# The overflow block of a mixture of experts, taken into the expert pairs: gate beside up in the two halves of the array

## The chip, the cores and the metric

The kernel runs on one core of one Trainium2 chip. The metric is the time of one execution on the device, in microseconds (us); lower is better. Of several runs the median counts.

## The reference

The model has two layers. Each mixes the tokens (attention beside a recurrent branch) and then sends every token through a hierarchical mixture of experts: 4 groups of 8 experts, the best group of a token, and the best two experts in it. In layer 0 all 512 tokens (256 of context, 256 latent) go through the experts, in layer 1 the 256 latent ones alone. The weights are of one layer; D_MODEL is 1024, an expert's hidden width 256, and everything is float32.

```
def hier_moe(h, w_rg, b_rg, w_re, b_re, w_e_gate, w_e_up, w_e_down):
...
    w_top = w_top / w_top.sum(-1, keepdims=True) * p_grp
    eid = grp[..., None] * EXPERTS_PER_GROUP + i_top
    comb = jnp.einsum('bnk,bnke->bne', w_top, jax.nn.one_hot(eid, N_EXPERTS, dtype=F32))
    y = jnp.zeros_like(h)
    for g in range(N_GROUPS):
        sl = slice(g * EXPERTS_PER_GROUP, (g + 1) * EXPERTS_PER_GROUP)
        a = jnp.einsum('bnd,edf->bnef', h, w_e_gate[sl])
        u = jnp.einsum('bnd,edf->bnef', h, w_e_up[sl])
        hid = jax.nn.silu(a) * u * comb[..., sl, None].astype(h.dtype)
        y = y + jnp.einsum('bnef,efd->bnd', hid, w_e_down[sl])
    return y
...
    for l in range(DEPTH):
...
            xc = layer_norm(DEEPNORM_ALPHA * xc + g2c * hier_moe(modulate(xc, sh2c, sc2c), *moe_args),
                            ln2_g[l], ln2_b[l])
        xl = layer_norm(DEEPNORM_ALPHA * xl + g2l * hier_moe(modulate(xl, sh2l, sc2l), *moe_args),
                        ln2_g[l], ln2_b[l])
```

## The kernel before, in words

Each layer is `mixer(l)` and then `moe(l)`. In `moe` every expert owns 64 slots, and a token takes a slot in each of its two experts. Tokens that find their expert full go to overflow blocks, 64 slots of one expert each; layer 0 always runs one such block, the first, and every further one stands behind a condition. Two experts make a pair. The weights of a pair, 6 MiB, lie in six tiles of 1 MiB: four of gate and up, two of down.

The loop over the 16 pairs j is written so that PE (TensorE) goes through it in the order of the code (`manual_schedule`). An iteration does this:

- `load` issues the four tiles of gate and up of pair j on SP's queue;
- `up` (L1438) multiplies the transposed tokens of both experts, 64 columns of the array for each, so that the matmuls of the two experts run abreast in the two halves of the array. A row of the program is one f32 matmul; in the trace it is two rows. The 512 output columns are gate and up side by side;
- `fetch(j + 2)`: `who` (L1426, DVE) finds which tokens are in the slots of the pair two further on, and `gather` (L1394, POOL) fetches them from HBM into one of three tiles `xr`;
- `finish` of the pair before: `place` builds the matrix Pm that puts slots back to tokens (L1415 and L1416, DVE), `load_down` issues its two tiles of down weights, and `down` (L1461) multiplies and splits the result into a high and a low part, yh (L189, ACT) and yl (L190, DVE);
- `turn(j + 1)` transposes the fetched tokens of the next pair (L1406, eight transposes);
- every second iteration `combine` begins for the two pairs finished by then: for each of 8 outputs (4 token tiles by 2 halves of D_MODEL) four matmuls, yh and yl of either pair (L1475, L1476), then DVE scales (L1478) and POOL adds to X (L1484). Four outputs are done in an iteration;
- `hidden` transposes the products silu(gate) times up (L1449).

After iteration j = 3 of layer 0 the block runs by itself: `extra(0, self.wm)` takes three weight tiles from the ring, fills them by indirect DMA on POOL's queue (L1347, tile `wx`), and goes through `who`, `gather`, `turn`, `up`, `hidden`, `down` and `combine` with one expert. Its `up` and `down` use one half of the array, and its `combine` is 16 matmuls over 64 slots.

The weight tiles go round in a ring, `self.wm`. It has four tiles of the whole kernel (`NW`) and `NW2` more during `moe`: 7 in layer 0 (11 in all), 9 in layer 1 (there the tile `X01` is taken in as well, 14 in all). A load waits until the tile that it overwrites has been read by its last matmul. The first loads of a layer are issued before the mixer has ended, as many as the ring has tiles.

After layer 0's experts, the weights `wada` of the next layer's modulation take over the ring (L382 multiplies by them), beside the layer norm of each token tile on DVE.

Of the kernel before, what the change touches and what calls it, by code (L numbers as in the profile page):

```python
# [83 lines left out]
class Kern:  # L84
# [199 lines left out]
    def run(self):  # L284
        tc, nc, I = self.tc, self.nc, self.I
        with ExitStack() as ctx:
            self.cp = ctx.enter_context(tc.tile_pool(name="const", bufs=1))
            self.wp = ctx.enter_context(tc.tile_pool(name="wslots", bufs=self.NW))
            self.dp = ctx.enter_context(tc.tile_pool(name="dram", bufs=1, space=bass.MemoryType.DRAM))
            self.cur = self.cp  # L290
            self.setup()
            for l in range(L):
                self.l = l
                self.PSB = {"g": 2, "a": 3, "t": 2, "d": 1}
                self.half, self.wi = None, -1
                self.NU = 34 if l == L - 1 else 40
                with tc.tile_pool(name=f"mix{l}", bufs=1, reuse_waits="tile") as self.mp, \
                        tc.tile_pool(name=f"psx{l}", bufs=1, space=bass.MemoryType.PSUM, reuse_waits="tile") as self.pp:
                    self.cur = self.mp
                    self.mixer(l)  # L300
                if self.stop == f"mix{l}":
                    return
                self.PSB = {"g": 1, "a": 2, "t": 2, "d": 3}
                self.NW2 = 9 if l == L - 1 else 7
                self.spare = [self.X01] if l == L - 1 else []
                with tc.tile_pool(name=f"moe{l}", bufs=1, reuse_waits="tile") as self.ep, \
                        tc.tile_pool(name=f"psm{l}", bufs=1, space=bass.MemoryType.PSUM, reuse_waits="tile") as self.pp:
                    self.cur = self.ep
                    self.moe(l)
                if self.stop == f"moe{l}":  # L310
                    return
# [984 lines left out]
    def moe(self, l):  # L1296
# [90 lines left out]
        def gather(tok, m, x=None):  # L1387

            ti = sm([128, 1], "ti", I32)
            if x is None:  # L1390
                x = xrs[xi[0] % 3]
                xi[0] += 1
            nc.vector.tensor_scalar(ti, tok, 512.0, None, op0=OP.add)
            nc.gpsimd.indirect_dma_start(out=x[0:m], out_offset=None, in_=self.h2_d[l],  # L1394
                                         in_offset=bass.IndirectOffsetOnAxis(ap=ti[0:m], axis=0),
                                         bounds_check=N - 1, oob_is_err=False)
            return x
# [69 lines left out]
        def combine(parts, sums=None):  # L1467

            for i, t in enumerate(QT):
                for h in range(2):  # L1470
                    hs = slice(h * 512, h * 512 + 512)
                    p = self.ps("d")
                    for j, (Pm, yh, yl, m) in enumerate(parts):
                        lt = Pm[0:m, i * 128:i * 128 + 128]
                        nc.tensor.matmul(p, lhsT=lt, rhs=yh[h][0:m], start=(j == 0), stop=False)  # L1475
                        nc.tensor.matmul(p, lhsT=lt, rhs=yl[h][0:m], start=False, stop=(j == len(parts) - 1))  # L1476
                    a = self.pm(name="acc") if sums else ep.tile([128, 512], F32, tag="acc", name="acc", bufs=2)
                    nc.vector.tensor_tensor(out=a, in0=p, in1=g2[t // 2][h], op=OP.mult)  # L1478
                    X = self.X[t][:, hs]
# [7 lines left out]
        def stats(X, nm, eps):  # L1487

            v, a, r = (self.ss_tile([128, 2], x) for x in "var")
            q, v, a, r = v[:, 1:2], v[:, 0:1], a[:, 0:1], r[:, 0:1]  # L1490
            xi[0] += 1
            nc.scalar.activation(xrs[xi[0] % 3], X, AF.Square, bias=nm, accum_out=q)
            nc.vector.tensor_scalar(v, q, 0.5 / D, 0.5 * eps, op0=OP.mult, op1=OP.add)
            self.newton(r, v, a)
            return r

        def extra(ob, new=None):

            W, Wd = load_indexed(ob, new)
            tok, ws = who(NSTAT + 64 * ob, "" if new else "x")  # L1500
            xs = turn(gather(tok, 64, None if new else xrs[2]), 64)
            yh, yl = down(hidden(up(xs, W, 1, ws), 1), Wd, 1)
            self.drain(combine([(place(NSTAT + 64 * ob), yh, yl, 64)]))

# [28 lines left out]
        got[1] = fetch(1)  # L1535
        with tc.manual_schedule(engines={eng.PE}):
            xs = turn(got[0][1], 128)
            for j in range(E // 2):
                W = load([2 * j, 2 * j + 1])
                ws, _ = got.pop(j)  # L1540
# [2 lines left out]
                    got[j + 2] = fetch(j + 2)  # L1543
                if hid:
                    finish(hid)
                if j + 1 < E // 2:
                    xs = turn(got[j + 1][1], 128)
                if len(done) == 2 or last and done and j == E // 2 - 1:
                    self.drain(comb)
                    comb = combine(done)  # L1550
                    done = []
                for _ in range(n):
                    next(comb, None)
                hid = hidden(si, 2), j
                if j == 3:
                    self.drain(comb)
                    if not last:
                        extra(0, self.wm)
        finish(hid)
        ln2 = self.wm("ln2")  # L1560
        for i, nm in enumerate(("ln2_g", "ln2_b")):
# [46 lines left out]
```

## Time and profile before

| | |
|---|---|
| median of 3 runs | 1428.43 us (1427.02 to 1432.36) |
| profiled execution | 1431.51 us, of which the span of the trace is 1429.4 us |
| mean granted TensorE clock | 0.947 of full speed |
| PE busy | 1294.4 us of the span |
| layer 0, experts | PE's first `up` at 541.88 us, last `combine` ends at 824.4 us |
| layer 1, experts | from 1177.3 us to the end |

Times in the trace count from the start of its span; the 2.1 us by which the execution is longer lie outside. PEclk in a row is the share of TensorE's full clock that was granted in that stretch; DMA is the mean busy share of the 16 DMA engines. In a timeline, a row is a run of like instructions: its start, its length from first start to last end, the engine, the line, the operation, the tile written and the tiles read, the shape and the count, and in square brackets the time for which the engine sat idle before and what ended that.

### The profile page before, as it was taken

The numbers are of one execution on the slowest core, as the hardware profiler recorded it, in microseconds if no ns is written. First come the engines' busy times: TensorE is split into PE (matmuls) and PEld (weight loads), VectorE is DVE, ScalarE is ACT, GpSimd is POOL, SyncE is SP. The second block draws the span as 40 slices with busy tenths as digits, with TensorE's granted clock in tenths as the row PEclk, the third lists the DMA queues.
The fourth block names the chain that finished last, engine by engine and source line by source line (L and its number), as shares of the span: only waits on it lengthen the run. The fifth ranks groups of instructions, "written<-read, shape, count | busy, mean of one in ns | idle before, by whom it ended". The sixth has DMA issues, their size and how long they took to land. (4 is left out here: it accounts for less than half of the span.)

```text
span 1429.4 us, 19667 instructions
## 1 busy us (share of the span) xinstructions
PE 1294.4 (91%) x6839; PEld 834.8 (58%) x6839; DVE 794.9 (56%) x2189; ACT 451.2 (32%) x998; POOL 377.7 (26%) x385
## 2 busy tenths in 40 slices
PE   5899999999999828999999959999999749999995
PEld 1788867776776623444454517898878634444342
DVE  3745777553236945555554486478775863343325
ACT  3534344443340102111121137356545212121121
POOL 1310114100343302444343212112524401232222
PEclk9999999999999858989999989999999959999998
DMA  9633464211247567979999968321444768999994
GB/s 326 207 114 131 145 214 140 82 30 59 89 177 269 168 256 250 403 264 409 408 407 409 403 211 278 96 81 39 152 143 132 237 250 329 408 408 406 407 409 158
DMA packets 145970, 339.64 MB, mean 238 GB/s; under 512 B 21552, under 2 KB 67792, under 8 KB 145856
## 3 DMA queue, kind: packets, MB, share of 16 engines
q1 hardware_dynamic: 137184, 322.61, 61.7%
q0 software_dynamic: 6224, 10.31, 2.1%
q10 hardware_dynamic: 2448, 5.31, 1.0%
q8 instruction: 59, 0.97, 0.3%
q14 instruction: 55, 0.45, 0.1%
HBM read 344.62 MB, written 4.29 MB: 244 GB/s over the span
## 5 line engine op out<-in xcount | busy, mean ns | idle before, releaser
L1438 PE MATMUL ps_g<-we,xs 128*64 128x512 f32 x992 | 243.7, 617 | 6.6 <-DMA we<-in_w_e_up 4.2
L1438 PEld LDWEIGHTS ps_g<-we,xs 128*64 128x64 f32 x992 | 76.3, 141 | 148.2 <-issue 141.6
L160 POOL TENSOR_TENSOR wsl<-wc,wsh 128x512 fp32r<-128x512 f32 x54 | 72.5, 1346 | 321.7 <-ACT wsh L176 284.1
L1484 POOL TENSOR_TENSOR X<-X,acc 128x512 f32<-128x512 f32 x96 | 125.2, 1327 | 109.8 <-DVE acc L1478 109.7
L160 DVE TENSOR_TENSOR wsl<-wc,wsh 128x512 fp32r<-128x512 f32 x108 | 84.5, 786 | 98.3 <-ACT wsh L176 87.0
L176 ACT ACTIVATE wsh<-wc 128x512 fp32r<-128x512 f32 x162 | 99.0, 628 | 118.6 <-PE ps_g L197 81.1
L1442 DVE SCALAR_TENSOR_TENSOR si<-si,ws,ps_g 128x256 f32<-128x256 f32 (+1 forms) x33 | 15.8, 480 | 211.4 <-ACT si L1441 211.4
L1461 PE MATMUL ps_a<-we,hidT 128*64 128x512 f32 x496 | 125.3, 595 | 2.1 <-DMA we<-in_w_e_down 1.9
L1394 POOL DMA_INDIRECT xr<-h2d,ti x33 | 34.9, 1057 | 315.2 <-PE ps_t L1406 207.2
L196 PE MATMUL ps_g<-hTh,wsh 128*128 128x512 f32 (+1 forms) x320 | 112.4, 351 | 2.0 <-ACT tg L639 2.0
L197 PE MATMUL ps_g<-hTl,wsh 128*128 128x512 f32 (+1 forms) x320 | 111.1, 347 | 0.0
L198 PE MATMUL ps_g<-hTh,wsl 128*128 128x512 f32 (+1 forms) x320 | 110.6, 346 | 0.0
L196 PE MATMUL ps_g<-wsh,hTh 128*128 128x256 f32 x368 | 105.5, 289 | 2.5 <-ACT v L599 2.4
L197 PE MATMUL ps_g<-wsl,hTh 128*128 128x256 f32 x368 | 104.2, 284 | 0.0
L198 PE MATMUL ps_g<-wsh,hTl 128*128 128x256 f32 x368 | 103.7, 283 | 0.0
L382 PE MATMUL ps_d<-wada,sT 128*32 128x512 f32 x380 | 70.3, 645 | 29.5 <-DMA wada<-in_w_ada 29.4
L1478 DVE TENSOR_TENSOR acc<-ps_d,g 128x512 f32<-128x512 f32 x108 | 74.1, 689 | 38.0 <-PE ps_d L1476 21.9
L1441 ACT ACTIVATE si<-ps_g 128x256 f32<-128x256 f32 (+1 forms) x33 | 12.7, 384 | 245.7 <-PE ps_g L1438 179.0
L1475 PE MATMUL ps_d<-yh,pmr 128*128 128x512 f32 (+1 forms) x200 | 83.7, 419 | 0.4 <-DVE acc L1478 0.2
L1461 PEld LDWEIGHTS ps_a<-we,hidT 128*64 128x64 f32 x496 | 38.6, 137 | 76.1 <-issue 62.8
L1476 PE MATMUL ps_d<-yl,pmr 128*128 128x512 f32 (+1 forms) x200 | 80.2, 403 | 0.9 <-DVE yl L190 0.9
L196 PEld LDWEIGHTS ps_g<-wsh,hTh 128*128 128x128 f32 x368 | 69.6, 190 | 9.2 <-ACT v L599 2.6
(420 smaller groups left out, 2710.3 us busy)
## 6 DMA issues: line engine op xcount, KB each, us to landing
we<-in_w_e_gate SPq DMA_DIRECT2D x124, 512.0 KB
we<-in_w_e_up SPq DMA_DIRECT2D x124, 512.0 KB
we<-in_w_e_down SPq DMA_DIRECT2D x124, 512.0 KB
wada<-in_w_ada SPq DMA_DIRECT2D x95, 512.0 KB
wc<-in_w_in SPq DMA_DIRECT2D x63, 512.0 KB
wc<-in_w_out SPq DMA_DIRECT2D x16, 512.0 KB
wc<-in_w_bo_mla SPq DMA_DIRECT2D x8, 512.0 KB
wc<-in_w_bo_mlstm SPq DMA_DIRECT2D x6, 512.0 KB
```

What stands on the lines that cost most here:

```text
L160: eng.tensor_tensor(out=out, in0=a, in1=b, op=OP.subtract)
L176: self.nc.scalar.activation(view(hi), src, AF.Copy)
L196: self.nc.tensor.matmul(out, lhsT=ah, rhs=bh, start=(i == 0), stop=False)
L197: self.nc.tensor.matmul(out, lhsT=ah, rhs=bl, start=False, stop=False)
L198: self.nc.tensor.matmul(out, lhsT=al, rhs=bh, start=False, stop=(i == n - 1))
L382: nc.tensor.matmul(ps[32 * c:32 * c + 32], lhsT=self.sT[:, kb], rhs=wt[c // 2][:, (c % 2) * 512:(c % 2) * 512 + 512], start=(kb == 0), sto ...
L1438: nc.tensor.matmul(p[64 * e:64 * e + 64], lhsT=xs[:, k, 64 * e:64 * e + 64], rhs=W[e, k], start=(k == 0), stop=(k == 7))
L1461: nc.tensor.matmul(p[64 * e:64 * e + 64], lhsT=hT_[:, c, 64 * e:64 * e + 64], rhs=W[e, c, h], start=(c == 0), stop=(c == 1))
L1475: nc.tensor.matmul(p, lhsT=lt, rhs=yh[h][0:m], start=(j == 0), stop=False)
L1476: nc.tensor.matmul(p, lhsT=lt, rhs=yl[h][0:m], start=False, stop=(j == len(parts) - 1))
L1478: nc.vector.tensor_tensor(out=a, in0=p, in1=g2[t // 2][h], op=OP.mult)
L1484: nc.gpsimd.tensor_tensor(out=X, in0=X, in1=a, op=OP.add)
```

## The change

The block of layer 0 is no longer a step of its own. A class `First` does its parts inside the iterations: `ask` (who and gather) in iteration 1, `place` and `up` in iteration 3 ahead of `hidden`, `down` in iteration 4 behind `finish`, and its result is a third part of the `combine` that starts in iteration 4. Its `up` puts gate (256 columns) into one half of the array and up into the other. Its `down` multiplies the same slots in both halves, so that the high part of the result lies in the rows 0 to 63 of one tile, and the low part in the rows 64 to 127; `combine` then needs one matmul over 128 rows for each output. The ring gets one tile more in either layer. The gathers of the pairs go round in two tiles `xr` in place of three, and the argument `dynamic_dma_scratch_size` is set to 4096.

```
-                self.NW2 = 9 if l == L - 1 else 7
+                self.NW2 = 10 if l == L - 1 else 8
...
-                x = xrs[xi[0] % 3]
+                x = xrs[xi[0] % 2]
...
-                        nc.tensor.matmul(p, lhsT=lt, rhs=yl[h][0:m], start=False, stop=(j == len(parts) - 1))
+                        end = j == len(parts) - 1
+                        nc.tensor.matmul(p, lhsT=lt, rhs=yh[h][0:m], start=(j == 0), stop=(end and yl is None))
+                        if yl is not None:
+                            nc.tensor.matmul(p, lhsT=lt, rhs=yl[h][0:m], start=False, stop=end)
...
+        class First:
+            def ask(o):
+                o.tok, o.ws = who(NSTAT, "x")
+                o.x = gather(o.tok, 64, xrs[2])
+
+            def place(o):
+                o.P = ep.tile([128, N], F32R, tag="pmx", name="pmx", bufs=1)
...
+            def up(o):
+                W, o.Wd = o.w
+                xs = turn(o.x, 64)
+                p = self.ps("a")
+                for k in range(8):
+                    for i in range(2):
+                        nc.tensor.matmul(p[64 * i:64 * i + 64, 0:256], lhsT=xs[:, k, 0:64], rhs=W[0, k][:, i],
+                                         start=(k == 0), stop=(k == 7))
+                o.si = sm([128, 256], "si", bufs=2)
+                nc.scalar.activation(o.si[0:64], p[0:64, 0:256], AF.Silu)
+                nc.vector.tensor_scalar(o.si[0:64], o.si[0:64], o.ws[0:64], None, op0=OP.mult)
+                nc.vector.tensor_copy(o.si[64:128], p[64:128, 0:256])
+
+            def down(o):
+                t = self.ps("t")
+                for c in range(2):
+                    nc.tensor.transpose(t[:, c * 128:c * 128 + 128], o.si[:, c:256:2], self.ident)
+                tv = t[:, 0:256].rearrange("p (c g s) -> p c g s", c=2, g=2)
+                hT_ = sm([128, 2, 128], "hidT", bufs=2)[:, :, 0:64]
+                nc.scalar.activation(hT_, tv[:, :, 0], AF.Copy)
+                nc.vector.tensor_tensor(out=hT_, in0=tv[:, :, 1], in1=hT_, op=OP.mult)
+                o.y = [self.st(F32R, "yx") for h in range(2)]
+                for h in range(2):
+                    p = self.ps("a")
+                    for c in range(2):
+                        for i in range(2):
+                            nc.tensor.matmul(p[64 * i:64 * i + 64], lhsT=hT_[:, c], rhs=o.Wd[0, c, h],
+                                             start=(c == 0), stop=(c == 1))
+                    y = o.y[h]
+                    nc.scalar.activation(y, p, AF.Copy)
+                    nc.vector.tensor_tensor(out=y[64:128], in0=p[64:128], in1=y[64:128].bitcast(F32), op=OP.subtract)
+                return o.P, o.y, None, 128
...
+            fb = None if last else First()
...
+                if fb and j == 1:
+                    fb.ask()
+                if fb and j == 4:
+                    done.append(fb.down())
...
-                if len(done) == 2 or last and done and j == E // 2 - 1:
+                if len(done) >= 2 or last and done and j == E // 2 - 1:
...
+                if fb and j == 3:
+                    fb.w = load_indexed(0, self.wm)
+                    fb.place()
+                    fb.up()
                 hid = hidden(si, 2), j
-                if j == 3:
-                    self.drain(comb)
-                    if not last:
-                        extra(0, self.wm)
...
-    nc = bacc.Bacc("TRN2", target_bir_lowering=False, num_devices=1)
+    nc = bacc.Bacc("TRN2", target_bir_lowering=False, num_devices=1, dynamic_dma_scratch_size=4096)
```

On PE, before, from `hidden` of pair 3 in layer 0 to `up` of pair 4 (after the last row shown, seven more outputs of the block's combine, two matmuls each, and then `up`):

```order
L1449 MATMUL ps_t<-ident,si 128x128 x2
L1406 MATMUL ps_t<-ident,xr 128x64 x8
L1438 MATMUL ps_g<-wx,xs 64x512 x8
L1449 MATMUL ps_t<-ident,si 128x64 x2
L1461 MATMUL ps_a<-wx,hidT 64x512 x4
L1475 MATMUL ps_d<-yh,pmr 128x512
L1476 MATMUL ps_d<-yl,pmr 128x512
```

On PE, of the change, from the block's `up` in iteration 3, behind its `turn`, to the first output of the combine in iteration 4 (L1476 and L1478 are the lines 1475 and 1476 of before):

```order
L1530 MATMUL ps_a<-wx,xs 64x256 x16
L1449 MATMUL ps_t<-ident,si 128x128 x2
L1438 MATMUL ps_g<-we,xs 64x512 x16
L1461 MATMUL ps_a<-we,hidT 64x512 x8
L1540 MATMUL ps_t<-ident,si 128x128 x2
L1550 MATMUL ps_a<-wx,hidT 64x512 x8
L1406 MATMUL ps_t<-ident,xr 128x128 x8
L1476 MATMUL ps_d<-yh,pmr 128x512
L1478 MATMUL ps_d<-yl,pmr 128x512
L1476 MATMUL ps_d<-yh,pmr 128x512
L1478 MATMUL ps_d<-yl,pmr 128x512
L1476 MATMUL ps_d<-yx,pmx 128x512
```

The block's `up` now stands ahead of `hidden` of pair 3, its `down` directly behind `down` of pair 3, and its share of the combine is a fifth matmul for each of 8 outputs (four in iteration 4, four in iteration 5).

On SP, before, the loads around the point where the tiles of the ring are used up for the first time in layer 0 (the branch belongs to the condition on further blocks; PE_49 is a wait for a matmul):

```order
L1320 DMA we<-in_w_e_gate 128x1024 [waits DMAHW0_49]
L1320 DMA we<-in_w_e_up 128x1024 [waits DMAHW1_49]
L1529 UNCONDITIONAL_BRANCH
L1320 DMA we<-in_w_e_gate 128x1024 [waits DMAHW2_49,PE_49]
L1320 DMA we<-in_w_e_up 128x1024 [waits DMAHW3_49]
```

On SP, of the change, the same place:

```order
L1320 DMA we<-in_w_e_gate 128x1024 [waits DMAHW0_49]
L1320 DMA we<-in_w_e_up 128x1024 [waits DMAHW1_49]
L1320 DMA we<-in_w_e_gate 128x1024 [waits DMAHW2_49]
L1320 DMA we<-in_w_e_up 128x1024 [waits DMAHW3_49]
L1581 UNCONDITIONAL_BRANCH
L1320 DMA we<-in_w_e_gate 128x1024 [waits DMAHW4_49,PE_49]
L1320 DMA we<-in_w_e_up 128x1024 [waits DMAHW5_49]
```

One gate and up tile more, two loads of 512 KB, stands ahead of the branch and waits for no matmul.

## Rows read from the trace of the kernel before

**Rows 1.** The page, first part: busy time of each engine.

```profile
PE 1294.4 (91%) x6839; PEld 834.8 (58%) x6839; DVE 794.9 (56%) x2189; ACT 451.2 (32%) x998; POOL 377.7 (26%) x385
```

**Rows 2.** Windows: us, busy time of five engines, PEclk, DMA share, GB/s.

```profile
634.05:797.45 163.40, 163.40 (x784) 80.91 (x780) 86.47 (x179) 33.17 (x65) 62.61 (x50) 1.00 1.03 404
...
824.40:860.40 36.00, 20.34 (x113) 4.53 (x112) 29.76 (x102) 12.65 (x24) 4.36 (x4) 0.81 0.64 221
...
1240.60:1400.80 160.20, 156.47 (x706) 67.63 (x704) 53.47 (x144) 31.52 (x63) 36.75 (x30) 1.00 1.03 407
```

**Rows 3.** Timeline of PE, pairs 3 to 5 of layer 0: start, length.

```profile
588.10 4.89 PE L1438 MATMUL ps_g<-we,xs 128*64 128x512 f32 x13 [2.03 <-DMA we<-in_w_e_up]
...
595.22 2.79 PE L1461 MATMUL ps_a<-we,hidT 128*64 128x512 f32 x10 [0.20 <-DMA we<-in_w_e_down]
...
602.97 1.26 PE L1406 MATMUL ps_t<-ident,xr 64*128 64x64 f32 x8
604.16 7.08 PE L1438 MATMUL ps_g<-wx,xs 128*64 128x512 f32 x16
...
624.66 9.55 PE L1438 MATMUL ps_g<-we,xs 128*64 128x512 f32 x32
634.05 3.60 PE L1461 MATMUL ps_a<-we,hidT 128*64 128x512 f32 x16
637.58 1.16 PE L1406 MATMUL ps_t<-ident,xr 128*128 128x128 f32 x8
638.50 0.47 PE L1475 MATMUL ps_d<-yh,pmr 128*128 128x512 f32 x1
...
642.30 0.39 PE L1449 MATMUL ps_t<-ident,si 128*128 128x128 f32 x2
642.62 3.65 PE L1438 MATMUL ps_g<-we,xs 128*64 128x512 f32 x16
```

**Rows 4.** Timeline of PE, the last pair of layer 0.

```profile
797.45 7.09 PE L1438 MATMUL ps_g<-we,xs 128*64 128x512 f32 x32
```

**Rows 5.** Windows of 10 us around the block, and one of 2.

```profile
620.00:630.00 10.00, 9.98 (x25) 4.06 (x25) 5.15 (x8) 0.00 (x0) 9.10 (x7) 0.52 0.21 84
630.00:640.00 10.00, 10.00 (x51) 4.41 (x48) 4.98 (x16) 2.67 (x5) 0.99 (x1) 1.00 0.79 245
590.00:592.00 2.00, 2.00 (x8) 0.80 (x6) 0.00 (x0) 0.00 (x0) 0.00 (x0) 0.50 1.04 305
```

**Rows 6.** Timeline of SP: weight loads issued, layer 0, then layer 1.

```profile
518.72 0.33 SPq L1320 DMA_DIRECT2D we<-in_w_e_up  x1
548.46 0.33 SPq L1320 DMA_DIRECT2D we<-in_w_e_gate  x1
...
782.09 0.33 SPq L1320 DMA_DIRECT2D we<-in_w_e_up  x1
...
1160.94 0.43 SPq L1320 DMA_DIRECT2D we<-in_w_e_up  x1
1183.61 1.75 SPq L1338 DMA_DIRECT2D we<-in_w_e_down  x4
```

**Rows 7.** Waits of PE from 541 to 860 us.

```profile
PE ps_d L382 <- DMA wada<-in_w_ada: 14.8, 4, 11.0
```

**Rows 8.** Timeline of DVE in the pair behind the block.

```profile
634.71 0.48 DVE L1442 SCALAR_TENSOR_TENSOR si<-si,ws,ps_g 128x256 f32<-128x256 f32 x1 [7.11 <-ACT si L1441]
...
638.75 0.69 DVE L190 TENSOR_TENSOR yl<-ps_a,yh 128x512 fp32r<-128x512 f32 x1
```

**Rows 9.** Groups by form, 640 to 797 us: weight loads of the pairs.

```profile
L1438 PEld LDWEIGHTS ps_g<-we,xs 128*64 128x64 f32 x320 | 22.1, 137 | 41.2 <-issue 40.0
```

**Rows 10.** Timeline of POOL, and the landing times of tile wx.

```profile
570.03 0.97 POOL L1347 DMA_INDIRECT wx<-in_w_e_gate,ridx  x1 [3.20 <-DMA we<-in_w_e_gate]
...
577.64 0.95 POOL L1347 DMA_INDIRECT wx<-in_w_e_down,ridx  x1 [0.30 <-issue]
...
DMA to landing us min/median/max: 9.6/10.9/12.2
```

More of the change, by code (lines that the diff above doesn't have):

```diff
@@ L1474, in combine @@
                         lt = Pm[0:m, i * 128:i * 128 + 128]
-                        nc.tensor.matmul(p, lhsT=lt, rhs=yh[h][0:m], start=(j == 0), stop=False)
-                        nc.tensor.matmul(p, lhsT=lt, rhs=yl[h][0:m], start=False, stop=(j == len(parts) - 1))
+                        end = j == len(parts) - 1
+                        nc.tensor.matmul(p, lhsT=lt, rhs=yh[h][0:m], start=(j == 0), stop=(end and yl is None))
+                        if yl is not None:
+                            nc.tensor.matmul(p, lhsT=lt, rhs=yl[h][0:m], start=False, stop=end)
                     a = self.pm(name="acc") if sums else ep.tile([128, 512], F32, tag="acc", name="acc", bufs=2)
@@ L1491, in stats @@
             xi[0] += 1
-            nc.scalar.activation(xrs[xi[0] % 3], X, AF.Square, bias=nm, accum_out=q)
+            nc.scalar.activation(xrs[xi[0] % 2], X, AF.Square, bias=nm, accum_out=q)
             nc.vector.tensor_scalar(v, q, 0.5 / D, 0.5 * eps, op0=OP.mult, op1=OP.add)
@@ L1503, in extra @@
             self.drain(combine([(place(NSTAT + 64 * ob), yh, yl, 64)]))
+        class First:
[4 more added lines that the diff above has]
+                o.P = ep.tile([128, N], F32R, tag="pmx", name="pmx", bufs=1)
+                s = sm([128, 1], "s0x", bufs=1)
+                for i in range(2):
+                    nc.gpsimd.memset(s[64 * i:64 * i + 64], float(NSTAT - 64 * i))
+                a = self.pm(name="pa")
+                nc.vector.tensor_scalar(a[:, 0:N], rows[:, 0, 0:N], s, None, op0=OP.is_equal)
+                nc.vector.scalar_tensor_tensor(o.P, rows[:, 1, 0:N], s, a[:, 0:N], op0=OP.is_equal, op1=OP.add)
+            def up(o):
[22 more added lines that the diff above has]
+                    for c in range(2):
+                        for i in range(2):
+                            nc.tensor.matmul(p[64 * i:64 * i + 64], lhsT=hT_[:, c], rhs=o.Wd[0, c, h],
[4 more added lines that the diff above has]
+                return o.P, o.y, None, 128
```

## The prediction

> **What bounds the kernel now.** The page gives PE 91% of the span [rows 1], so the first question is whether PE waits for something in the stage that is changed or is itself the bound. The windows by stage answer it: from 634 to 797 us (layer 0's pairs behind the block) PE is busy for 163.40 of 163.40 us at full clock, and the DMA engines are full too, at 404 GB/s [rows 2]. The timeline gives the period: ten pairs lie between 642.62 and 797.45 us, 15.48 us each [rows 3, 4]. A pair's 6 MiB at 404 GB/s take 15.57 us, so PE and DMA are all but level, and the question is who leads. The block decides it. Ahead of it PE waits for weights: 2.03 us in `up` of pair 3, and until 595.22 us for the down weights of pair 2 [rows 3]. Then the block runs alone from 602.97 to 624.66 us, and DMA, which goes on, fills the ring and stands: 84 GB/s from 620 to 630 us, 245 from 630 to 640 [rows 5]. From then on DMA is ahead and PE is the bound: the last load of gate and up of pair 15 is issued at 782.09 [rows 6], 15.4 us before PE wants it [rows 4].
>
> Behind layer 0's experts there is a tail of 36 us in which PE works for 20.3 [rows 2] and waits 14.8 us for `wada` [rows 7]; all of it hangs on the last pairs and should move with them. In layer 1 DMA is full from 1240 to 1401 us, at 407 GB/s [rows 2]: there DMA is the bound, and before it it stood still because the ring was full, with no load issued between 1160.94 and 1183.61 us [rows 6].
>
> **What goes.** The block's own stage, 624.66 − 602.97 = 21.69 us [rows 3]. Behind it TensorE ran at half clock (0.52 granted from 620 to 630 us [rows 5]), and `up` of pair 4 took 9.55 us [rows 3] where that of pair 15 takes 7.09 [rows 4]: 2.46 more. Together 24.15 us.
>
> **What comes on PE.** In iteration 3:
> - eight transposes, 604.16 − 602.97 = 1.19 us [rows 3];
> - the block's `up`. It has 32 rows in the trace's count, of 256 columns in one half. In a pair 32 rows of 512 columns, two halves abreast, take 7.09 us, 0.222 each [rows 4]; half the columns give 32 × 0.111 = 3.55 us. No row shows 256 columns. If the weight loads, 137 ns each [rows 9], set the pace, it is 32 × 0.137 = 4.38; if the halves don't run abreast, it is the 7.08 of the block before [rows 3]. I take 3.55: the rows of a pair show both halves abreast.
>
> The Trainium skill ("TensorE: Matmul & The Clock Gate", LDWEIGHTS) has a load cost its columns over 1.2, in ns: 53 for 64 columns. The trace shows 137, so by the page alone the loads would never set the pace of 111, and by the trace they could; that is 0.8 us in the sum.
>
> In iteration 4, behind `down` of pair 3:
> - two transposes of 128x128, as `hidden` of a pair has them: 642.62 − 642.30 = 0.32 us [rows 3];
> - a stall that was not there. `down` needs hidT, and its last factor comes from a DVE multiplication that stands in DVE's queue behind yl of pair 3. In before that yl starts at 638.75 and takes 0.69 us [rows 8], while `down` of pair 3 gave PE free at 637.58 [rows 3]. The multiplication is not in the trace; by the nearest (L1442, 128x256 in 0.48 [rows 8]) it takes about 0.4. So hidT is ready at about 639.9, PE has its transposes done at 637.9, and the stall is 2.0 us. Behind it on PE stand the block's `down`, `turn(5)` and the combine;
> - what a stall does to the clock. After the 2.03 us wait of pair 3 the granted clock was 0.50 at 590 to 592 us [rows 5], and 13 rows took 4.89 us [rows 3] where 0.222 each and the last one's 0.6 give 3.3. I take 1.5 for it; the bounds are 0 and the 2.46 above;
> - `down` in both halves, 16 rows as in a pair: 637.58 − 634.05 = 3.53 us [rows 3];
> - in iterations 4 and 5 eight matmuls of combine more. Sixteen take 642.30 − 638.50 = 3.80 us [rows 3], so 1.90.
>
> The sum is 1.19 + 3.55 + 0.32 + 2.0 + 1.5 + 3.53 + 1.90 = 13.99 us, and the saving 24.15 − 13.99 = 10.2 us. The rest of the block is as before or less (one share of 8 scalings and additions to X on DVE and POOL falls away) and lies beside PE's pairs.
>
> A page speaks against such mixing: the Trainium skill ("TensorEngine Tiling (Array Packing)", Key Properties) says that a change of tiling mode drains TensorE, and `down`, transposes, `down`, `turn` change it twice more. In the trace `turn(5)` starts 3.53 us after a `down` of 16 rows of 0.222, that is without a gap, so I charge nothing.
>
> **What the tile brings.** The order shows two loads of 512 KB more ahead of the first wait for a matmul. In layer 0 the queue stood from 518.72 to 548.46 us [rows 6]; a tile loaded there puts every later weight 1.05 MB ahead, 2.6 us at 404 GB/s. Until 595 us PE follows the weights, so it gains that: 2.6 us. Not more, because the half clock at 590 us lies ahead of the wait at 595.22 [rows 3] and costs nothing there; not less than 0. In layer 1 the tile falls into the hole from 1160.94 to 1183.61 [rows 6], and the bound stretch ends 2.6 us earlier. Both depend on tiles alone.
>
> **Does DMA allow it?** PE will be ahead by 10.2 + 2.6 us. DMA stood for about 10 × (404 − 84)/404 + 10 × (404 − 245)/404 = 7.9 + 3.9 = 11.9 us behind the block [rows 5]. A block that is 10.2 us shorter leaves 1.7 of them, and the lead of 15.4 us at pair 15 stays. DMA does not become the bound in layer 0, but by little.
>
> The block's weights: six gathers go out from 570.03 to 578.6 and land 9.6 to 12.2 us later [rows 10], by 591; PE will want them at about 600. Gathers of tokens in two tiles instead of three, and `dynamic_dma_scratch_size`, I cost at nothing: a gather may go once `turn` two pairs earlier has read its tile, and has a pair's period of 15.48 us [rows 3, 4] to land. If that cover is gone, see the fourth rival.
>
> **The sum:** 10.2 + 2.6 + 2.6 = 15.4 us off the profiled 1431.51: 1416.1. That run lies 3.1 us above the median of the runs shown, 1428.43; on the median it is 1413.0.
>
> **The rivals.**
> 1. *The block costs more than that.* Halves not abreast or weight loads at the pace (up to 7.08 for 3.55 [rows 3]), a half clock of 2.5 instead of 1.5 us, and tiles that bring 1 instead of 2.6 us in layer 0 because the wait moves to another tile: 15.4 − 3.5 − 1.0 − 1.6 = 9.3, so 1419. For it: no row of 256 columns, and a stall of the same length did halve the clock. Against: 32 rows abreast at 0.222.
> 2. *The tail closes up.* PE's 14.8 us of waits for `wada` [rows 7] shrink because those loads find DMA earlier free, or the stall does not touch the clock: 4 to 8 us more, about 1407. For it: the DMA share in the tail is only 0.64 [rows 2]. Against: the loads wait for tiles that PE frees and DVE is busy for 29.8 of 36 us [rows 2].
> 3. *The gain is eaten.* DMA, level with PE, loses time in its queue (the gathers of `wx` share it), and PE waits in pairs 4 and 5 for what the block no longer hides. Then layer 0 keeps some 3 us and layer 1 its 2.6: 1423, within 0.5%. For it: 1.7 us of standing left. Against: PE's 15.48 us a pair against DMA's 15.57 cost DMA's lead only 0.1 us a pair from there on.
> 4. *Slower, by POOL's queue.* POOL issues the six gathers 1.3 us apart without waiting for one to land (570.03 to 577.64 [rows 10]). If the smaller scratch makes each wait for the landing of the one before, they take 6 × 10.9 = 65 us instead of 8.6, the block's weights come at 570 + 65 = 635 in place of 600, and with them the additions to X queued behind: 35 us lost against 15.4 gained, about 1448. It decides from 26 us of delay (15.4, and 10 of margin on the landing). Against: each gather's own rows of work are few, and nothing in the trace shows POOL short of room.
>
> **How the numbers follow.** What a measurement can tell from no change is 0.5%, 7.1 us. My forecast (10 to 18 us less, 1410 to 1418) has a chance of 0.62, the first rival 0.18, the second 0.11, the third 0.05, the fourth 0.04. The range leaves out the third and the fourth and the far ends of the first two: 1406 to 1420.5. Faster takes the forecast, the second and the first (9.3 is beyond 7.1, but its lower edge is not: 0.02 go to the same): 0.89; same 0.07; slower 0.04.
>
> **What would show it.** Right: `up` of the block 3.6 us with 32 rows; an idle of PE of about 2 us between its two transposes and its `down`, put down to DVE; combine in steps of five; `up` of pair 4 in 7.1 us, or at half clock not for long; a pair's period of 15.5 us to the end; DMA standing for about 2 us after the block; layer 1's pairs with the same period and an end 2.6 us earlier counted from its first `up`. Wrong: PE waits for `wx`, or for weights after pair 5; gathers on POOL further apart; `up` of 7 us; a tail other than 36 us.

## The result, and the profile after

The changed kernel took 1413.61 us (median of 4 runs, 1411.23 to 1415.03) against 1428.36 us before (median of 4 runs by now): a ratio of 0.9885, with a 95% interval of 0.9868 to 0.9903, that is 13.9 to 18.9 us less. A second measurement, beside the experiments below, gave 0.9871 (0.9851 to 0.9891), 15.6 to 21.3 us less. The forecast of 1413.0 corresponds to 0.9892. The two profiled executions lie 20.0 us apart in their spans (1429.4 and 1409.4); that is more than the medians differ, and the ledger further down shows where they lie.

The timeline of PE in the changed kernel, from the down of pair 2 to the up of pair 5 (columns as in [rows 3]):

```profile
587.37 2.79 PE L1461 MATMUL ps_a<-we,hidT 128*64 128x512 f32 x10 [1.17 <-DMA we<-in_w_e_down]
590.09 1.15 PE L1406 MATMUL ps_t<-ident,xr 128*128 128x128 f32 x8
...
594.89 1.09 PE L1406 MATMUL ps_t<-ident,xr 64*128 64x64 f32 x8
596.08 3.67 PE L1530 MATMUL ps_a<-wx,xs 128*64 128x256 f32 x32
599.68 0.51 PE L1449 MATMUL ps_t<-ident,si 128*128 128x128 f32 x2
600.12 7.09 PE L1438 MATMUL ps_g<-we,xs 128*64 128x512 f32 x32
607.04 3.60 PE L1461 MATMUL ps_a<-we,hidT 128*64 128x512 f32 x16
610.57 0.51 PE L1540 MATMUL ps_t<-ident,si 128*128 128x128 f32 x2
612.68 3.65 PE L1550 MATMUL ps_a<-wx,hidT 128*64 128x512 f32 x16 [1.60 <-DVE hidT L1544]
616.26 1.16 PE L1406 MATMUL ps_t<-ident,xr 128*128 128x128 f32 x8
617.18 0.48 PE L1476 MATMUL ps_d<-yh,pmr 128*128 128x512 f32 x1
...
621.91 0.40 PE L1449 MATMUL ps_t<-ident,si 128*128 128x128 f32 x2
622.24 7.09 PE L1438 MATMUL ps_g<-we,xs 128*64 128x512 f32 x32
```

The reader can go through the sum with it. Iteration 3 now takes 596.08 − 594.89 = 1.19 us for the block's turn and 599.68 − 596.08 = 3.60 for its up; iteration 4 takes 612.68 − 610.57 = 2.11 for the two transposes and the stall of 1.60, and 616.26 − 612.68 = 3.58 for the block's down; the combine takes 621.91 − 617.18 = 4.73 where [rows 3] had 3.80, so 0.93 more, twice. The up of pair 4 starts 10.0 us after the turn of pair 4, where it started 26.7 us after it before (the turn of before stands with the ledger).

Windows of the changed kernel (columns as in [rows 2]): two microseconds at the stall, twenty where DMA stood before [rows 5], and the tail:

```profile
612.00:614.00 2.00, 1.32 (x6) 0.48 (x8) 0.62 (x2) 0.00 (x0) 0.00 (x0) 1.00 1.03 410
620.00:630.00 10.00, 10.00 (x47) 4.37 (x48) 2.12 (x4) 0.77 (x2) 4.52 (x4) 1.00 1.03 407
630.00:640.00 10.00, 10.00 (x52) 6.18 (x50) 8.24 (x19) 2.67 (x5) 5.12 (x4) 1.00 1.03 408
804.89:840.85 35.96, 18.67 (x109) 4.24 (x108) 30.05 (x102) 12.70 (x24) 4.37 (x4) 0.81 0.62 219
```

The granted clock stays at 1.00 through the stall, where the prediction had 1.5 us of loss by half clock. DMA moves 407 and 408 GB/s where it moved 84 and 245: it no longer stands at all. The tail is 36 us as before [rows 2]. PE's waits from 541 to 860 us (columns as in [rows 7]) show the same wait for `wada`, about as long, and the one new wait:

```profile
PE ps_d L382 <- DMA wada<-in_w_ada: 16.1, 7, 14.1
PE ps_a L1550 <- DVE hidT L1544: 1.6, 1, 1.6
```

It is the end of this chain, on DVE:

```profile
611.74 0.68 DVE L190 TENSOR_TENSOR yl<-ps_a,yh 128x512 fp32r<-128x512 f32 x1
612.34 0.28 DVE L1544 TENSOR_TENSOR hidT<-ps_t,hidT 128x128 f32<-128x128 f32 x1
```

The multiplication L1544 starts when yl of pair 3 lets it, as forecast, takes 0.28 us, and 0.06 us behind it the block's down begins. More than yl stands ahead of it: from 607.70 us, when the product of pair 4 comes (L1442), DVE works on `who`, `place` and yl without a gap, so all of that is in the stall.

The weight loads on SP, in layer 0, at its last pair, and in layer 1 (columns as in [rows 6]):

```profile
517.58 0.33 SPq L1320 DMA_DIRECT2D we<-in_w_e_up  x1
544.31 0.33 SPq L1320 DMA_DIRECT2D we<-in_w_e_gate  x1
...
764.14 0.33 SPq L1320 DMA_DIRECT2D we<-in_w_e_up  x1
...
1144.51 0.45 SPq L1320 DMA_DIRECT2D we<-in_w_e_up  x1
1165.34 0.80 SPq L1338 DMA_DIRECT2D we<-in_w_e_down  x2
```

In either layer the queue still stands once, from 517.58 to 544.31 and from 1144.51 to 1165.34 us, with one tile more in the ring. The last load of gate and up of pair 15 goes out 13.8 us ahead of its up at 777.97; it was 15.4 [rows 6, 4].

And POOL's gathers of the block's weights (as in [rows 10]):

```profile
565.84 0.97 POOL L1347 DMA_INDIRECT wx<-in_w_e_gate,ridx  x1 [3.39 <-PE ps_g L1438]
...
572.45 1.25 POOL L1347 DMA_INDIRECT wx<-in_w_e_down,ridx  x1 [0.30 <-issue]
...
DMA to landing us min/median/max: 7.4/10.6/13.6
```

They still follow one another by 1.3 us and land within 13.6 us, at 587 at the latest, 9 us before PE wants them.

**A ledger.** Four stretches can be read from the timelines of every run: from the first up of layer 0 to the turn of pair 4 (what lies ahead of the block), from there to the up of pair 6 (the block), from the first to the last up of layer 0 (both, and nine undisturbed pairs more), and from the first up of layer 1 to the end of the span. For the kernel before, the first up is that of 541.88 us, and the waits, the turn of pair 4 and the up of pair 6 are these (columns as in [rows 3]):

```profile
593.94 1.08 PE L1461 MATMUL ps_a<-we,hidT 128*64 128x512 f32 x4 [0.49 <-DMA we<-in_w_e_down]
...
597.94 1.15 PE L1406 MATMUL ps_t<-ident,xr 128*128 128x128 f32 x8
...
658.12 7.09 PE L1438 MATMUL ps_g<-we,xs 128*64 128x512 f32 x32
```

In us (each stretch comes from one profiled execution, each median from 4 to 12 runs):

| run | median | ahead of block | block | layer 0, first to last up | layer 1 |
|---|---|---|---|---|---|
| before | 1428.36 | 56.06 | 60.18 | 255.57 | 252.09 |
| after | 1413.61 | 50.89 | 48.56 | 238.77 | 249.36 |
| e1_after_again | 1413.29 | 50.54 | 48.56 | 238.42 | 249.79 |
| e2_no_tiles | 1421.25 | 55.55 | 50.50 | 245.38 | 252.68 |
| e3_up_one_half | 1417.07 | 52.77 | 51.96 | 244.05 | 250.94 |
| e4_early_hidden | 1413.15 | 52.59 | 47.21 | 239.12 | 249.99 |
| e7_combine_64 | 1420.41 | 51.56 | 53.53 | 244.41 | 250.38 |
| e8_more_ring | 1413.72 | 52.41 | 47.20 | 238.93 | 248.81 |
| e9_before_tiles_b | 1425.75 | 52.63 | 60.19 | 252.14 | 250.15 |
| e10_before_room_b | 1430.79 | 55.12 | 59.08 | 253.53 | 252.75 |
| e11_longer_stall | 1417.63 | 51.77 | 51.47 | 242.56 | 249.38 |
| e12_block_later | 1414.97 | 49.21 | | 238.63 | 252.12 |

What the table leaves out is the mixer of layer 0 (first up at 539.2 to 543.1 us in these runs) and everything from the last up of layer 0 to the first of layer 1 (379.9 to 387.5 us). Both wander by some us from run to run, with before-like and changed kernels mixed: 379.9, 385.7 and 382.5 us for before, e9 and e10, 382.1 and 386.0 for the changed kernel's two profiles. Between the two profiled executions they differ by little: the first up is 2.7 us earlier and the part between the layers 2.2 us longer, so 19.5 of the 20.0 us lie in the experts, 16.8 in layer 0 and 2.7 in layer 1. That is more than the terms below add up to (17.8), chiefly because the stretch ahead of the block is the longest of the table in that execution of before and among the shortest in that of after. The kernel before was measured beside each group: 1431.44 us beside e1 to e4, 1431.83 beside e5 to e8, 1429.79 beside e9 to e12, so medians are compared within a group.

### The profile page after: what moved, and what is told of

Its sections match the earlier page's. It is cut to its first block, busy times and chain, and to the rows that moved or that the text cites. A ratio compares the mean times of both kernels' runs of the same rounds, so it can differ in the third digit from the quotient of the medians.

```text
span 1409.4 us, 19658 instructions
## 1 busy us (share of the span) xinstructions
PE 1273.7 (90%) x6855; PEld 826.8 (59%) x6855; DVE 790.1 (56%) x2183; ACT 451.6 (32%) x998; POOL 368.0 (26%) x379
## 4 chain that ended last, share of the span: by engine, by line
PE 39%; DMA 21%; DVE 10%; issue 2%; ACT 2%; SPq 0%; ACTq 0%; DVEq 0%; POOL 0%; POOLq 0%
DMA we<-in_w_e_up 10%; PE ps_g L1438 7%; DMA we<-in_w_e_down 7%; PE ps_g L196 6%; PE ps_g L198 6%; PE ps_g L197 6%; PE ps_a L1461 4%; PE ps_d L1476 2%; PE ps_d L1478 2%; DMA X<-in_w_e_up 1%; PE ps_t L1406 1%; PE ps_a L1106 1%; PE ps_a L934 1%; DVE ln_r L154 1%; DMA h2d<-h 1%
## 5 line engine op out<-in xcount | busy, mean ns | idle before, releaser
L1438 PE MATMUL ps_g<-we,xs 128*64 128x512 f32 x1000 | 235.3, 602 | 4.6 <-ACT xs L1408 2.3
L1486 POOL TENSOR_TENSOR X<-X,acc 128x512 f32<-128x512 f32 x88 | 114.8, 1326 | 87.9 <-DVE acc L1480 86.2
L1442 DVE SCALAR_TENSOR_TENSOR si<-si,ws,ps_g 128x256 f32<-128x256 f32 x32 | 15.4, 481 | 193.8 <-ACT si L1441 193.8
L1480 DVE TENSOR_TENSOR acc<-ps_d,g 128x512 f32<-128x512 f32 x100 | 68.7, 690 | 35.1 <-PE ps_d L1478 20.6
L1441 ACT ACTIVATE si<-ps_g 128x256 f32<-128x256 f32 x32 | 12.3, 384 | 219.6 <-PE ps_g L1438 179.5
L1476 PE MATMUL ps_d<-yh,pmr 128*128 128x512 f32 x192 | 78.9, 412 | 0.4 <-DVE acc L1480 0.2
L1478 PE MATMUL ps_d<-yl,pmr 128*128 128x512 f32 x192 | 75.6, 395 | 0.0
```

The source lines that it names most:

```text
L1438: nc.tensor.matmul(p[64 * e:64 * e + 64], lhsT=xs[:, k, 64 * e:64 * e + 64], rhs=W[e, k], start=(k == 0), stop=(k == 7))
L1486: nc.gpsimd.tensor_tensor(out=X, in0=X, in1=a, op=OP.add)
```

## The experiments

**e1: the changed kernel again.**

> The changed kernel once more, as the yardstick for the runs beside it. Theory 1 (the terms of the prediction, as the trace of the changed kernel corrects them: block 11.6 us, tile in layer 0 2.6, tile in layer 1 2.6, nothing else): 13 to 17 us under the kernel before. Theory 2 (the 20 us between the two profiled spans are real, and the tail or the mixers gave some of it): 18 us or more.

It took 1413.29 us beside 1431.44 of the kernel before, 18.2 us less; the block's stretch is 48.56 us again. The terms read from the traces give 11.6 + 3.7 + 2.5 = 17.8 (below). By the number alone that is theory 2's. But in the ledger and around it nothing else gained: the tail is as long as before, and from the last up of layer 0 to the first of layer 1 this execution took 386.0 us, 6.1 more than that of before. So theory 1's terms stand, with a larger tile in layer 0. The two measurements of the same pair of kernels, 14.8 and 18.2 us, show how far such a difference is known: their intervals overlap, and both hold 17.8.

**e2: without the tiles.**

```
-                self.NW2 = 10 if l == L - 1 else 8
+                self.NW2 = 9 if l == L - 1 else 7
```

> The changed kernel with the ring as it was, 11 and 14 tiles. Theory 1 (a tile is worth the 2.6 us in which DMA loads it while it would stand, in either layer): 5 us over the changed kernel, half of it in the pairs before the block as waits for weights (about 2.7 us of them), half between the first up of layer 1 and the end. Theory 2 (in layer 0 the wait only moves, or PE's clock takes it): 2.6 us over it, all in layer 1. Theory 3 (the tiles bring nothing): within 1 us.

1421.25 us, 8.0 more than e1: theory 1 in kind, and more than its 5. It is 10.2 us less than the kernel before: that is the block without the tiles. In layer 1 it lost 2.9 us (252.68 against 249.79), ahead of the block 5.0, and in the block 1.9. The timeline of PE of this run and a window (columns as above) show why:

```profile
590.01 5.11 PE L1461 MATMUL ps_a<-we,hidT 128*64 128x512 f32 x14 [2.97 <-DMA we<-in_w_e_down]
...
635.60 1.08 PE L1461 MATMUL ps_a<-we,hidT 128*64 128x512 f32 x4 [0.49 <-DMA we<-in_w_e_down]
636.88 2.79 PE L1461 MATMUL ps_a<-we,hidT 128*64 128x512 f32 x10 [0.20 <-DMA we<-in_w_e_down]
```

```profile
590.00:600.00 10.00, 9.99 (x39) 5.33 (x40) 3.63 (x9) 2.28 (x4) 3.00 (x3) 0.85 1.02 408
```

PE waits 2.97 us for the down weights of pair 2, then goes on at a mean granted clock of 0.85, so that 14 rows of down take 5.11 us. And it catches up with DMA a second time, in the down of pair 4, which takes 639.60 − 634.09 = 5.5 us with its two waits instead of 3.5. Before, with the same ring, there was no such wait: the old block took 21.7 us, in which DMA got ahead.

**e3: the block's up in one half.**

```
-                    for i in range(2):
-                        nc.tensor.matmul(p[64 * i:64 * i + 64, 0:256], lhsT=xs[:, k, 0:64], rhs=W[0, k][:, i],
-                                         start=(k == 0), stop=(k == 7))
+                    nc.tensor.matmul(p[0:64], lhsT=xs[:, k, 0:64], rhs=W[0, k], start=(k == 0), stop=(k == 7))
...
-                nc.vector.tensor_copy(o.si[64:128], p[64:128, 0:256])
+                nc.vector.tensor_copy(o.si[64:128], p[0:64, 256:512])
```

> The changed kernel, but the block's up in one half of the array with 512 columns, gate and up in a row as before. Theory 1 (two halves with 256 columns are abreast, and PE is the bound here): up takes 7.1 us instead of 3.67, and the kernel is 3.4 us slower. Theory 2 (PE has slack here, since weights come late again): less than 1.5 us slower.

```profile
601.83 7.08 PE L1529 MATMUL ps_a<-wx,xs 128*64 128x512 f32 x16
608.84 0.51 PE L1449 MATMUL ps_t<-ident,si 128*128 128x128 f32 x2
```

The up takes 7.08 us, the block's stretch 51.96, that is 3.40 more than 48.56, and the median is 3.8 us over e1. Theory 1 holds: what PE spends more in this place shows in full in the stretch, and the median agrees within its noise.

**e4: the stall taken away.** The two transposes and the product stand in a step of their own, `hid`, ahead of `finish`, and the block's down behind `turn`:

```
+                if fb and j == 4:
+                    fb.hid()
                 if hid:
                     finish(hid)
...
-                if fb and j == 4:
-                    done.append(fb.down())
                 if j + 1 < E // 2:
                     xs = turn(got[j + 1][1], 128)
+                if fb and j == 4:
+                    done.append(fb.down())
```

> The changed kernel, but the block's two transposes and the product hidT stand ahead of the down of pair 3, and the turn of pair 5 ahead of the block's down. Theory 1 (the stall of 1.60 us before the block's down is DVE's queue, and PE is the bound behind it): the stall falls to 0.3 us or less, and the kernel is 1.3 to 1.6 us faster. Theory 2 (what PE gains here it gives back to weights that are not there, since DMA never stands any more): no gain, and waits for weights appear in pairs 5 to 15.

```profile
609.00 0.51 PE L1540 MATMUL ps_t<-ident,si 128*128 128x128 f32 x2
609.43 3.65 PE L1461 MATMUL ps_a<-we,hidT 128*64 128x512 f32 x16
613.02 1.15 PE L1406 MATMUL ps_t<-ident,xr 128*128 128x128 f32 x8
614.09 3.65 PE L1554 MATMUL ps_a<-wx,hidT 128*64 128x512 f32 x16
617.68 0.50 PE L1476 MATMUL ps_d<-yh,pmr 128*128 128x512 f32 x1
```

No row has a wait any more, and the block's stretch is 47.21 us, 1.35 less. No wait for weights appears in pairs 5 to 15, so theory 1 holds in the trace. In the median (1413.15 against 1413.29) it does not show: the stretch ahead of the block happened to be 2 us longer in the profiled execution, and 0.1% is less than these medians can tell.

**e5 and e6: two runs that don't count.** They were to be the kernel before with the tiles, and with the room alone. But the block's own gather went round in the two tiles with those of the pairs, so that pair 5 got the tokens of pair 6, and PE waited 2.77 us for the block's gather in e5.

> The kernel before, with the block by itself behind pair 3, but with the ring of the change (12 and 15 tiles), two tiles for the gathers of the pairs and the scratch of 4096. Theory 1 (the tile's gain in layer 0 is a gain of its own, since PE follows the weights until the down of pair 2): 4 to 7 us under the kernel before, 2.4 of it in layer 1. Theory 2 (in layer 0 the tile is worth something only together with the shorter block, since the ring fills behind the old block anyway): 2.4 us under the kernel before, all in layer 1. Either way: if the mixer of layer 1 again takes 320 us and more from its first transposes to the first up, where the profile of before has 318, the added 3 us belong to the room that was made, and not to the block.

> The kernel before with what makes room alone: two tiles for the gathers of the pairs instead of three, and the scratch of 4096, the ring as it was. Theory 1 (gathers and scratch cost nothing): within 1.5 us of the kernel before, six gathers of the block's weights still 1.3 us apart. Theory 2 (fourth rival of the prediction: they wait for one another): 20 us and more above it. Theory 3 (they cost something in the mixer of layer 1): 2 to 4 us above it.

They took 0.9985 and 1.0020 of the kernel before. With that wait in them (2.98 us in e6) the times tell neither theory from the other. What lies ahead of the block is not touched by it: 49.87 us with the tile (e5) and 55.12 without (e6), which fits the runs of the ledger. e9 and e10 are the same two kernels with the block's gather in the third tile.

**e7: the block's result in two tiles of 64 rows.**

```
-                o.y = [self.st(F32R, "yx") for h in range(2)]
...
-                return o.P, o.y, None, 128
+                yh, yl = down(hT_, o.Wd, 1)
+                return o.P, yh, yl, 64
```

> The changed kernel, but the block's down in one half of the array and its result split into a high and a low tile of 64 rows, so that its share of the combine is two matmuls for each output instead of one. Theory 1 (the terms of the prediction): down takes 3.5 us as in both halves, the combines of iterations 4 and 5 take 1.9 us more, and the kernel is 1.9 us slower. Theory 2 (POOL's additions to X or DVE's scalings set the pace of these combines): no slower.

1420.41 us, 11.4 less than the kernel before, where e1 had 18.2. The block's stretch is 53.53, 5.0 more than 48.56, where theory 1 had 1.9; the medians of the two groups differ by 6.8, which is the same within their noise. Down took 3.58 us, as expected. The first output of the combine on PE (columns as above; each output is four matmuls over 128 rows and two over 64):

```profile
620.79 0.48 PE L1476 MATMUL ps_d<-yh,pmr 128*128 128x512 f32 x1
621.11 0.39 PE L1478 MATMUL ps_d<-yl,pmr 128*128 128x512 f32 x1
621.34 0.39 PE L1476 MATMUL ps_d<-yh,pmr 128*128 128x512 f32 x1
621.57 0.40 PE L1478 MATMUL ps_d<-yl,pmr 128*128 128x512 f32 x1
621.89 0.49 PE L1476 MATMUL ps_d<-yh,pmx 64*128 64x512 f32 x1
622.23 0.39 PE L1478 MATMUL ps_d<-yl,pmx 64*128 64x512 f32 x1
622.55 0.50 PE L1476 MATMUL ps_d<-yh,pmr 128*128 128x512 f32 x1
622.89 0.39 PE L1478 MATMUL ps_d<-yl,pmr 128*128 128x512 f32 x1
```

From start to start, matmuls of one kind follow each other by 0.23 us. Where the rows change from 128 to 64, 621.57 to 621.89 and the next, and back, 622.23 to 622.55 and the next, it is 0.32, 0.34, 0.32, 0.34. Four steps an output of 0.10 us too much, in eight outputs, are 3.2 us, and eight matmuls of 0.23 more are 1.8: 5.0. The rows show the delay and where it comes; what the engine does in it they don't show.

**e8: one tile more in layer 1,** on the kernel of e4.

```
-                self.NW2 = 10 if l == L - 1 else 8
+                self.NW2 = 11 if l == L - 1 else 8
...
+        xrs = [ep.tile([128, D], F32, tag=f"xr{i}", name="xr", bufs=1) for i in range(2 if l == L - 1 else 3)]
```

> The kernel of run e4_early_hidden (the block's hidT early, turn of pair 5 ahead of its down) with one more tile in the ring of layer 1, 16 in all; the place for it is the third tile of the gathers, which layer 1 does without. Theory 1 (DMA still stands for 20 us ahead of the first up of layer 1, so every tile there is worth 2.6 us): the stretch from the first up of layer 1 to its last down falls by another 2.4 to 2.6 us, to about 225.4, and the kernel is 2.5 us under e4_early_hidden and the fastest of all. Theory 2 (the pairs of layer 1 can't take the tile earlier, PE being the bound there by now): no change.

Layer 1 took 248.81 us in the trace, 1.2 less than in e4 and not 2.5; the median, 1413.72, is no better than e1's. This is neither theory. By this one execution the tile is worth something, but less than the one before it. That is not shown: runs with the ring of the change spread from 249.36 to 252.12, and the medians have no gain.

**e9: the tiles on the kernel before.** The edit is the change's own lines for the ring, the gathers and the scratch, with the block as it was, its gather in `xrs[2]`.

> The kernel before with the ring of the change (12 and 15 tiles), two tiles for the gathers of the pairs, the third for the block's own gather, and the scratch of 4096. Theory 1 (the tile of layer 0 is worth 4 to 5 us by itself, since PE follows the weights until the down of pair 2, and 2.4 in layer 1): 5 to 7.5 us under the kernel before; down of pair 2 ends 51 to 53 us behind the first up instead of 56. Theory 2 (it is worth something in layer 0 only with the shorter block): 2.4 us under the kernel before.

1425.75 us against 1429.79, a ratio of 0.9975 (0.9959 to 0.9991), 4.0 us: theory 1 by the stretches (52.63 us ahead of the block, 250.15 in layer 1), though the median falls short of its 5. Its interval, 1.3 to 5.9 us, holds theory 2's 2.4 as well, so it is the stretches that decide. The profiled execution is one of the slowest of the twelve (1431.52 us). Of PE's waits from 540 to 800 us, the one for weights is

```profile
PE ps_a L1461 <- DMA we<-in_w_e_down: 1.2, 1, 1.2
```

where the kernel before waited 2.03 and 0.20 us [rows 3] and 0.49 between them (shown with the ledger). The block's stretch is 60.19, that of before: the tile shows no gain there.

**e10: the room alone.**

> The kernel before with what makes room alone: two tiles for the gathers of the pairs, the third for the block's own, and the scratch of 4096; the ring as it was. Theory 1 (this costs nothing): within 1.5 us of the kernel before. Theory 2 (gathers wait for one another or for their tiles): 4 us and more above it, with waits of PE for gathered tokens in layer 0's pairs.

1430.79 against 1429.79, a ratio of 1.0006 (0.9994 to 1.0017): gathers in two tiles and the smaller scratch cost nothing that shows, 2.4 us at most. The fourth rival is out.

**e11: a longer stall.**

```
                 nc.vector.tensor_tensor(out=hT_, in0=tv[:, :, 1], in1=hT_, op=OP.mult)
+                for _ in range(5):
+                    nc.vector.tensor_scalar(hT_, hT_, 1.0, None, op0=OP.mult)
```

> The changed kernel with five more DVE operations (each a multiplication of hidT by 1) between hidT and the block's down, so that PE's stall there is about 3 us instead of 1.60. Theory 1 (the prediction's 1.5 us for the clock were right for a longer stall, and the real one was too short): the granted clock falls to half behind the stall, and the way from down of pair 3 to up of pair 5 takes 1.4 us more for the stall and 1 to 2.5 us for the clock. Theory 2 (a stall here does not touch the clock): 1.4 us more and no half clock.

PE's timeline and two windows:

```profile
615.64 5.24 PE L1552 MATMUL ps_a<-wx,hidT 128*64 128x512 f32 x16 [2.95 <-issue]
```

```profile
616.00:618.00 2.00, 2.00 (x6) 0.53 (x4) 0.00 (x0) 0.00 (x0) 0.00 (x0) 0.50 1.05 418
618.00:620.00 2.00, 2.00 (x10) 0.73 (x8) 0.17 (x1) 0.60 (x1) 0.00 (x0) 0.78 1.01 399
```

The profile names no releaser for this idle time; on DVE the five multiplications end at 615.54, 0.10 us ahead of the down. The stall is 2.95 us, 1.35 more; behind it the granted clock is 0.50 and 0.78, and the block's down takes 5.24 us where it took 3.65. The stretch is 51.47 us, 2.9 over 48.56, which is 1.35 for the stall and 1.6 for the clock. Theory 1.

**e12: the block two iterations later,** on the kernel of e4.

```
-                if fb and j == 1:
+                if fb and j == 3:
...
-                if fb and j == 3:
+                if fb and j == 5:
```

and 6 for 4 in both places of down.

> The kernel of run e4_early_hidden with every part of the block two iterations later (up in 5, down in 6), so that its weights are gathered behind those of pair 3. Theory 1 (ahead of pair 3 PE follows DMA, and 3 MiB of the block's weights there cost it up to 2 us): the waits for weights in pairs 2 and 3 go, and the stretch from first to last up of layer 0 falls by 1 to 3 us. Theory 2 (the block's time is what lets DMA get ahead, so without it in iterations 3 and 4 the waits only move to pairs 3 to 5): within 1 us of e4_early_hidden.

PE's waits from 540 to 800 us:

```profile
PE ps_a L1461 <- DMA we<-in_w_e_down: 1.0, 1, 1.0
PE ps_t L1449 <- ACT xs L1408: 0.6, 2, 0.3
PE ps_d L1476 <- DVE acc L1480: 0.6, 1, 0.6
```

The stretch to the turn of pair 4 is down to 49.21 us, the shortest of all; but a wait of 1.0 us for down weights is still there, and one of 0.6 for the scaling in the combine, and from first to last up it is 238.63 us against 239.12 in e4. What it gained ahead, 3.4 us against e4, it gave back there: the down of pair 4 takes 623.27 − 617.72 = 5.55 us with its wait, where one without takes 3.53, and the iteration of pair 4, with the wait in the combine, takes 16.30 us instead of 15.48. Theory 2: the waits move, and the sum stays. The median, 1414.97, is not below the others.

## Why the prediction was right, point by point

- **What bounds.** PE in layer 0 behind the block, DMA ahead of it and in layer 1: shown by e3 and e11, where PE's time in the block counts in full (3.4 and 2.9 us), and by e2 and e9 for the weights. Nine pairs from 6 to 15 take 139.3 us in every run that has the block ahead of them.
- **The block.** The forecast was 10.2 us; the stretch fell by 60.18 − 48.56 = 11.6. The terms from the trace after: turn 1.19 (1.19 forecast), up 3.60 (3.55), the transposes and the stall 2.11 (2.32), down 3.58 (3.53), combine 1.86 (1.90), the half clock 0 (1.5). They add up to 12.34, so 11.8 of the 24.15 are saved; 0.12 of the rest is in the transposes of `hidden` behind the block's up (last section). Gate beside up with 256 columns does run at half the 7.08: the weight loads did not set the pace, nor did the halves take turns. The first rival's reasons are out.
- **The stall's clock was mis-sized:** "I take 1.5 for it; the bounds are 0 and the 2.46 above". It was 0: behind the 1.60 us of the real stall the clock did not fall. That a longer stall in this place has such a price e11 shows (1.6 us behind 2.95); no run has a stall of the forecast 2.0 us.
- **The tile in layer 0 was mis-sized too:** "so it gains that: 2.6 us. Not more". The stretch ahead of the block is 51.9 us in the mean of the eight runs with the tile (after, e1, e3, e4, e7, e8, e9 and e11) and 55.6 in the mean of the three without (before, e2, e10): 3.7 us. Of these 3.5 lie between the up of pair 3 and the turn of pair 4, which take 10.45 us where PE waits for nothing (e12), 2.5 more in the mean of the eight and 6.0 more in that of the three; 0.3 is a first up that happened to be longer in the three. And part of the 3.5 is the clock: without the tile PE waits 2.7 to 3.7 us in all for weights and then goes on at half clock, with it 0.3 to 2.2 us, and in all eight the granted clock stays at 1.00 in the windows of 10 us from 580 to 610 us. The step that failed is that the half clock at 590 us "lies ahead of the wait at 595.22" and costs nothing. That holds for the one execution it was read from; in e2 and e10 the slow rows lie behind the last wait (in e2 14 rows of down in 5.11 us), and their loss counts.
- **And it was costed as if it were alone.** I wrote that the tiles' gain depends "on tiles alone". Without them the shorter block loses 1.9 us to a second wait in pair 4 (50.50 against 48.56 us, in the one execution of e2 that was profiled), which is the third rival's mechanism. The medians point the same way but don't show it: the tiles brought 4.0 us to the kernel before (e9, 1.3 to 5.9) and 8.0 us to the changed one (e2 against e1), yet the block alone (e2, 10.2 us) and the tiles alone (e9, 4.0) add up to 14.2, and the first measurement of both together is 14.8.
- **Layer 1:** 2.6 forecast. 252.5 us in the mean without the tile (before, e2, e10), 250.0 in that of the runs just named with it, leaving out e8, which has one more: 2.5. e12 has the tile and 252.12, which I can't explain; with it the mean is 250.3 and the difference 2.2.
- **Does DMA allow it?** I had DMA stand for 1.7 us more behind the block; it did not stand. A block that saves 11.6 instead of 10.2 us leaves 0.3 of the 11.9 us for which DMA stood, and the tile put PE ahead by 3.7 us instead of 2.6. The lead at pair 15 fell from 15.4 to 13.8 us.
- **The tail** moved as a whole: 36 us, and 16.1 us of waits for `wada` instead of 14.8. The second rival came by its other half alone, the stall that does not touch the clock, and that is worth 1.5 us and not its 4 to 8.
- **POOL** showed no delay, and e10 shows it for the room.

Both misses, 1.5 for the clock and 1.1 for the tile, make the gain larger than forecast, and both lie within the bounds of the range. So it is in part luck that the forecast of 1413.0 lies 0.6 us from the median: by the terms as the traces show them it would have been 1410.6. The medians can't tell the two apart, since the first measurement's 13.9 to 18.9 us hold both the forecast's 15.4 and the 17.8. Its difference from the second (14.8 and 18.2 us) is within the noise of the two; no run took it apart.

## What to carry to other kernels

Where PE and DMA take the same time for a step, ask what a special step in between gives the other engine: the old block's time let DMA get ahead for good, and with the ring as it was, 1.9 of the 11.6 us saved by shortening it went into a new wait for weights (e2, one execution). Cost such a pair of edits together, and try each without the other. And pack a small operand so that it has the shape of its neighbours: the block's high and low part stacked to 128 rows saved 5.0 us of combine against two tiles of 64 rows, of which the fewer matmuls were only 1.8.

## What was unexpected of the hardware

Going from matmuls over 128 rows to matmuls over 64 and back delayed two steps at each change by some 0.10 us (e7). The Trainium skill ("TensorEngine Tiling (Array Packing)", Key Properties) states that changing the tiling mode drains TensorE. The prediction charged nothing for that because `turn(5)` started on time after `down`; e7 agrees with the page, and so does the row at 599.68 us after (that a drain is the cause, neither shows): the two transposes of `hidden` behind the block's up take 0.44 us until the next up starts, where those behind a combine take 0.32 [rows 3].

The first up of layer 0 ran at half clock for a different time in each execution: the granted clock is 0.50 until 541 us in after and until 547 us in before, and the up takes 8.54 and 10.02 us, where one at full clock takes 7.09. It is 8.46 us in e1 and 9.71 in e3, and that makes 1.25 of the 2.2 us by which the stretch ahead of the block differs between these two (50.54 and 52.77), which are alike there. DMA's loads restart when this up frees its first tiles, 5.1 us behind its start in after and 6.6 in before. The rest of the 2.2 us is in the waits for weights, and those don't follow the first up: e7 has the longest, 10.13 us, and the shortest wait of the eight.
